# Recurrence steps traced 1000 places ahead of their own from the second group's round on, in a one-core decoder layer

## The chip, the cores and the metric

The program runs on one core of a Trainium2 chip. That core has a matrix engine (PE, with its weight loads shown apart as PEld), a vector engine (DVE), a scalar engine (ACT), a general engine (POOL) and a queue from which nearly all DMA transfers are issued (SP). Each engine works through its own instructions in the order in which the program lists them. The metric is the time of one execution in microseconds (us); lower is better. A difference of about 0.3%, some 10 us here, is the least that the measurement can tell from no change.

## What is computed

One decoder layer is applied to 1024 prompt positions and to 8 x 4 sample positions. Only the parts that matter here:

```python
z = rmsnorm(x) @ w_in
y_r = rwkv7_mix(z[..., :D_SHIFT], ...)    # a recurrence over positions
y_p = pool_mix(z[..., D_SHIFT:], ...)
h = x + concat([y_r, y_p]) @ w_out
h = h + peer_ffn(rmsnorm(h))              # top 16 of 16384 experts for each of 8 heads
h = h + (p @ ple_w) * sigmoid(rmsnorm(h) @ ple_gate_w)
y = rmsnorm(h)
```

The recurrence keeps a 64 x 64 state for each of 8 heads and updates it at every position, `s = s * w + s_kk (kk*a) + v k`, so it is serial along the prompt. `peer_ffn` projects to queries, scores them against two key tables, takes the best pairs, and sums the chosen experts' values with their gates.

## The kernel before

**Phase A** projects all 1056 positions and leaves the recurrence's inputs in DRAM (`fd`).

**The recurrence** is cut into 16 chunks of 64 prompt positions (`bchunk`, 17 calls with the sample positions). A chunk loads its inputs (`fdc`, L481), forms products and masks (`lp`, L492), inverts a triangular matrix by repeated products (`ltm`, `zp`, `yx`), takes the state of the chunk before it (`s_in = S[-1]`), writes a new state `S` (L595, L596), and normalizes and stores its rows (`yo` L617, `y_d` L619). Its matmuls are all recorded at L470. It is a Python generator of about 19 steps. `b_stream(ca, cb)` runs up to three chunks at a time (`NSLOT`), the next one started at least six steps (`STAG`) after the last, and it may start chunks up to two beyond `cb`.

**Phase C** (`phase_c(gi)`) takes one group of positions (`GROUPS`: 0..288, 288..544, 544..800, 800..1056): it loads `y_d` (L683), applies `w_out` (8 blocks), stores `h` and its normalized halves (`xh_d`, `xl_d`), applies `wq` (16 blocks) and the keys, and stores the scores `sc_d` (L743). Its matmuls are at L653 to L655, their weights come from `wc_d` (L642, L643) after the first group. Its tiles have one buffer, so the groups' phases run one after another. Chunks 0 to 3 belong to the first group with the sample positions, 4 to 7 to the second, 8 to 11 to the third, 12 to 15 to the fourth.

**The top stream** (`t_stream(gi)`) covers the first 672 positions in tiles of up to 128: it loads scores (`scq`, L758), picks the best on DVE (L761 to L766, `select`), and spreads the gates into a dense matrix: comparisons and products `ab` on DVE and POOL (L901, L902, L904), matmuls at L912, evictions `gst` on ACT (L913), and 2 MB stores `g_d` (L915).

**Rounds.** `merge` interleaves the streams in the trace, the one with the smallest finished share next. `BC = (0, 2, 4, 5, 8, 12, 16)` sets the chunks of each call: chunks 0 to 4 are traced beside the end of phase A, the sample positions and the pool's projection. Then come four rounds:

| round | recurrence | top stream | phase C |
|---|---|---|---|
| 1 | chunks 5 to 7 | | first group |
| 2 | 8 to 11 | first group | second group |
| 3 | 12 to 15 | second group | third group |
| 4 | | third group, up to 672 | fourth group, with 8 blocks of the dense stage |

After round 3 the recurrence's pools are closed (`pbx.close()`), and the dense stage's buffers (`dr`, `dps`) take their space: the loads of `XH` and `XL` (L1156, L1157), the first expert weights (`eraw<-uT`, L1092) and the dense matmuls (L1118) come behind the last chunk.

**The dense stage** works through all 16384 experts for the first 672 positions. Its first blocks need `XH` and `XL` only; the rest need the gates `gq` (from `g_d`), so the last `g_d` store of the third group. Beside it DVE and POOL gather experts for the last 384 positions.

**The order on each engine** is made when the program is built. Each instruction has a priority, its place in the trace; a planner runs a model of the chip's times, and whenever an engine is free there, it gives it the ready instruction with the smallest place. An instruction that isn't ready is passed over. What comes out is a fixed list for each engine and for the SP queue. `tc.high_priority(offset=n)` lowers the place of everything traced inside it by n.

Of the kernel before, what the change touches and what calls it, by code (L numbers as in the profile page):

```python
# [63 lines left out]
def body(ctx, tc, io):  # L64
# [852 lines left out]
    NG = len(GROUPS)  # L917
    NSLOT = 3
    STAG = 6

    active, nxt, since, held = [], [0], [0], [False]

    def b_stream(ca, cb, ahead=2):
        while nxt[0] < cb or any(c < cb for c, _ in active):
            c = nxt[0]
            if (c < min(cb + ahead, NCH) and len(active) < NSLOT and (not active or since[0] >= STAG)
                    and not (held[0] and c % NSLOT == 1)):
                active.append((c, bchunk(c)))
                nxt[0], since[0] = c + 1, 0
            since[0] += 1  # L930
            for a in list(active):
                try:
                    next(a[1])
                except StopIteration:
                    active.remove(a)
                yield

    def b_len(ca, cb):
# [29 lines left out]
    BC = (0, 2, 4, 5, 8, 12, 16)  # L968
    with tc.tile_pool(name="pa1", bufs=1) as pa1:
        with tc.tile_pool(name="pa", bufs=1) as pa:  # L970
            A = phase_a(pa1, pa)
            while next(A) is None:
                pass
        pb = pbx.enter_context(tc.tile_pool(name="pb", bufs=1, side="right", reuse_waits="tile"))
        id16 = pb.tile([128, 4, 64], F16, name="id16")
        for i in range(4):
            ACT(id16[:, i, :], ident2, AF.Copy)
        S = [pb.tile([128, 4, 64], F32, name="S", bufs=3)]

        def bzero():  # L980
            nc.gpsimd.memset(S[0], 0.0)

        bzero()
        merge([(16, A), (b_len(*BC[0:2]), b_stream(*BC[0:2]))])

    with tc.tile_pool(name="smp", bufs=1) as sp_, tc.tile_pool(name="hx", bufs=1) as hx:
# [67 lines left out]
        spf = sp_.tile([128, 28, 64], F32, name="spf")  # L1054
        nc.gpsimd.memset(spf, 0.0)
        merge([(30, sample(bchunk(-1, ((sp_, ssm), bmask, cmask, spf)))), (b_len(*BC[1:3]), b_stream(*BC[1:3]))])
        merge([(KB * (1 + T // XW), (x for st in (ple(), wpool()) for x in st)), (b_len(*BC[2:4]), b_stream(*BC[2:4]))])


# [343 lines left out]
def program(arrays, extra=()):  # L1403
    nc = bacc.Bacc("TRN2", target_bir_lowering=False, num_devices=1)
    io = {k: nc.dram_tensor(k, v.shape, mybir.dt.from_np(v.dtype), kind="ExternalInput").ap()
          for k, v in arrays.items()}
    for k, s in list(OUTS.items()) + list(extra):
        io[k] = nc.dram_tensor(k, s, F32, kind="ExternalOutput").ap()
    with tile.TileContext(nc, schedule_with_timeline_sim=True) as tc, ExitStack() as ctx:
        body(ctx, tc, io)  # L1410
    return nc
# [15 lines left out]
```

## Time and profile before

| | us |
|---|---|
| median of three runs | 3326.09 |
| lowest, highest of them | 3318.22, 3327.06 |
| the execution that was profiled | 3320.66 |
| its span, first to last instruction | 3318.5 |

A profile page shows each engine's busy time as a share of the span. A table of windows shows the same for stretches of the span, with the granted PE clock as a share of full speed and the share of the DMA engines' time in use. A chain of waits is followed back from the last instruction: each piece is what the next one waited for. In a timeline, the square bracket gives the idle time of the engine before a row and what ended it. The stages of the span:

| us from the start | stage |
|---|---|
| 0 to 520 | phase A, pool, sample positions, chunks 0 to 4 |
| 520 to 1350 | the four rounds, chunks 5 to 15 |
| 1350 to 3158 | dense stage |
| 3158 to 3318.5 | output stage |

### The profile page before, as it was taken

Reading aid. Unit: us, or ns where it says so; the run is one execution under the profiler, and the core shown is the slowest. Engines: PE = TensorE matmul, PEld = TensorE weight load, DVE = VectorE, ACT = ScalarE, POOL = GpSimd, SP = SyncE. Lnnn points to the kernel's source line nnn. Section 1 sums busy time; section 2 is a strip of 40 time slices with the busy share of each in tenths; the row PEclk is TensorE's granted clock in tenths of the full one; section 3 lists DMA queues with packets and bytes.
Section 4 is the critical chain, followed back from the end, with each engine's and each line's share of the span. In section 5 each row is a group of like instructions: output and inputs, shape, how many; then the busy total and the mean of one; then the engine's idle time right before and its main releaser. Section 6 shows DMA issues by size and latency. Waiting matters only on the chain.

```text
span 3318.5 us, 66499 instructions
## 1 busy us (share of the span) xinstructions
PE 3129.6 (94%) x26777; PEld 3000.2 (90%) x26777; DVE 2576.9 (78%) x4930; ACT 1129.7 (34%) x1732; POOL 1705.2 (51%) x1366
## 2 busy tenths in 40 slices
PE   8998898987988888999999999999999999999997
PEld 7886787876877787999999999999999999999997
DVE  7775333469599888789888888888888888888966
ACT  6442423434454555432222122222222222212243
POOL 5212232235464465247666665666566666666534
PEclk9999899988998988999999999999999999999998
DMA  3325557855776987559999899999999989999833
GB/s 117 117 87 128 149 142 230 278 176 173 213 214 200 282 260 224 198 209 350 341 350 328 325 354 331 328 343 339 330 336 353 329 326 341 333 332 340 309 109 127
DMA packets 437333, 858.89 MB, mean 259 GB/s; under 512 B 108960, under 2 KB 232096, under 8 KB 432544
## 3 DMA queue, kind: packets, MB, share of 16 engines
q1 hardware_dynamic: 326432, 451.93, 41.6%
q0 software_dynamic: 110592, 402.70, 33.0%
q8 instruction: 210, 3.44, 0.4%
q14 instruction: 99, 0.81, 0.1%
HBM read 733.92 MB, written 120.60 MB: 258 GB/s over the span
## 4 chain that ended last, share of the span: by engine, by line
PE 75%; DVE 12%; DMA 5%; issue 2%; ACT 2%; POOL 2%; SPq 1%; ACTq 0%; DVEq 0%; POOLq 0%
PE pd L1118 58%; PE ps L470 5%; PE ps L219 4%; DVE ab L901 2%; PE ps L653 2%; PE ps L655 2%; PE ps L654 2%; PE ps L302 1%; DMA whi<-wc_d 1%; PE ps L912 1%; DVE ab L902 1%; POOL ab L127 1%; DMA scq<-sc_d 1%; DVE ab L904 1%; DMA sc_d<-scs 1%
## 5 line engine op out<-in xcount | busy, mean ns | idle before, releaser
L1227 POOL DMA_INDIRECT row<-v,idx x384 | 542.9, 1414 | 313.7 <-DVE po L1244 154.0
L1227 POOL DMA_INDIRECT row<-u,idx x384 | 543.7, 1416 | 282.8 <-DVE row L1235 123.0
L1094 ACT ACTIVATE ehi<-eraw 128x1024 fp32r<-128x1024 f32 x278 | 294.9, 1061 | 1109.3 <-PE pd L1118 999.9
L1118 PE MATMUL pd<-XH,elo 128*128 128x336 f32 x2176 | 513.8, 317 | 2.4 <-DVE elo L1096 2.2
L1118 PE MATMUL pd<-XL,ehi 128*128 128x336 f32 x2176 | 514.4, 317 | 0.0
L1118 PE MATMUL pd<-XH,ehi 128*128 128x336 f32 x2176 | 512.5, 316 | 0.7 <-ACT ehi L1094 0.7
L1118 PE MATMUL pd<-wh,ehi 128*128 128x336 f32 (+1 forms) x2112 | 504.0, 317 | 6.3 <-DVE tg L1308 6.3
L1118 PE MATMUL pd<-wh,elo 128*128 128x336 f32 (+1 forms) x2112 | 503.9, 317 | 0.0
L1118 PE MATMUL pd<-wl,ehi 128*128 128x336 f32 (+1 forms) x2112 | 502.7, 317 | 0.0
L1244 DVE SCALAR_TENSOR_TENSOR po<-row,act,po 128x1024 f32<-128x1024 f32 x381 | 488.5, 1282 | 6.6 <-DMA row<-v,idx 0.2
L1235 DVE SCALAR_TENSOR_TENSOR row<-row,xt 128x1024 f32<-128x1024 f32 x384 | 455.0, 1219 | 8.3 <-DMA row<-u,idx 8.3
L1096 DVE TENSOR_TENSOR elo<-eraw,ehi 128x1024 fp32r<-128x1024 f32 x256 | 318.5, 1244 | 73.8 <-ACT ehi L1094 63.2
L1118 PEld LDWEIGHTS pd<-XH,elo 128*128 128x128 f32 x2176 | 373.0, 188 | 3.1 <-DVE elo L1096 2.7
L1118 PEld LDWEIGHTS pd<-XH,ehi 128*128 128x128 f32 x2176 | 372.7, 189 | 1.2 <-ACT ehi L1094 0.9
L1118 PEld LDWEIGHTS pd<-XL,ehi 128*128 128x128 f32 x2176 | 371.4, 188 | 0.2
L1118 PEld LDWEIGHTS pd<-wh,ehi 128*128 128x128 f32 x2112 | 362.5, 188 | 7.1 <-issue 6.9
L1118 PEld LDWEIGHTS pd<-wl,ehi 128*128 128x128 f32 x2112 | 362.7, 188 | 0.0
L1118 PEld LDWEIGHTS pd<-wh,elo 128*128 128x128 f32 x2112 | 361.9, 188 | 0.2
L653 PE MATMUL ps<-hi,whi 128*128 128x256 f32 (+1 forms) x592 | 189.1, 321 | 46.0 <-DMA whi<-wc_d 24.2
L1187 DVE TENSOR_TENSOR OT<-pd,OT 128x672 f32<-128x672 f32 x120 | 102.9, 858 | 148.5 <-PE pd L1118 147.5
L127 POOL TENSOR_TENSOR ab<-ab,e 128x512 f16<-128x512 f16 x110 | 143.5, 1317 | 135.3 <-DVE ab L902 96.4
L913 ACT ACTIVATE gst<-ps 128x512 f32<-128x512 f32 x168 | 174.2, 1098 | 94.9 <-PE ps L912 89.9
(427 smaller groups left out, 5431.2 us busy)
## 6 DMA issues: line engine op xcount, KB each, us to landing
eraw<-uT SPq DMA_DIRECT2D x128, 512.0 KB
eraw<-vP SPq DMA_DIRECT2D x128, 512.0 KB
g_d<-gst SPq DMA_DIRECT2D x21, 2048.0 KB
gq<-g_d SPq DMA_DIRECT2D x32, 1344.0 KB
whi<-wc_d SPq DMA_DIRECT2D x108, 256.0 KB
wlo<-wc_d SPq DMA_DIRECT2D x108, 256.0 KB
fdc<-fd SPq DMA_DIRECT2D x16, 896.0 KB
wc_d<-whi SPq DMA_DIRECT2D x40, 256.0 KB
```

The lines of the kernel that those rows point to most:

```text
L127: nc.gpsimd.tensor_tensor(out, a, b, op=op)
L219: mm(ps[:, :XW], s[:, k, :], x[:, k, a:b], start=first, stop=last)
L470: mm(o[hs], l[hs], r[hs], start=start, stop=stop)
L653: mm(ps[:, :n], whi[:, kk, :], xhi[:, k, :n], start=k == 0, stop=False)
L913: ACT(st[:, :, t2 + q:t2 + q + 4].rearrange("p e t -> p t e"), v3(ps, 128), AF.Copy, scale=1.0 / GS)
L1094: ACT(hi, raw, AF.Copy)
L1096: sub(lo, raw, hi.bitcast(F32), op=ALU.subtract)
L1118: mm(ps[:, a, :n], w_[:, k, :], x_[:, s:s + n], start=first, stop=last)
L1187: TT(halves(OT[db]), ps[:, :, :NH], halves(OT[db]), op=ALU.add)
L1227: nc.gpsimd.indirect_dma_start(out=r[:m], out_offset=None, in_=io[tab], in_offset=bass.IndirectOffsetOnAxis(ap=idx[:m, hh, k:k + 1], axis=0))
L1235: STT(r[:m], r[:m], 1.0, xt[:m], op0=ALU.mult, op1=ALU.mult, accum_out=pre[:m, k:k + 1])
L1244: STT(po[:m], r[:m], act[:m, k:k + 1], po[:m], op0=ALU.mult, op1=ALU.add)
```

## The change

`b_stream` gets a `with` around each single step of a chunk. For calls with `ca >= BC[3]` (= 5), so rounds 1 to 3, everything that the step traces (its matmuls, its work on DVE, ACT and POOL, its load of `fdc` and its store of `y_d`) has a place 1000 smaller than its own. The three calls before (chunks 0 to 4, and those steps of chunks 5 and 6 that these calls start ahead) keep their places, and so does every instruction of the other streams. `next(a[1], 0) == 0` is the end of the generator, as the caught `StopIteration` was. The order of the trace, the buffers, the arithmetic and the dependences are as before.

```diff
     STAG = 6
+    LEAD = 1000
...
             for a in list(active):
-                try:
-                    next(a[1])
-                except StopIteration:
-                    active.remove(a)
+                with tc.high_priority(offset=LEAD) if ca >= BC[3] else nullcontext():
+                    if next(a[1], 0) == 0:
+                        active.remove(a)
                 yield
```

## Prediction

> **What bounds the kernel now.** I read the table of windows first, to see which engine is full in which stage.
>
> ```profile
> core 0: us, PE busy (x) PEld busy (x) DVE busy (x) ACT busy (x) POOL busy (x), PEclk, DMA share, GB/s
> 520.00:690.00 170.00, 149.62 (x2286) 137.64 (x2282) 68.34 (x195) 69.79 (x151) 40.74 (x51) 0.93 0.82 268
> 690.00:850.00 160.00, 126.22 (x1790) 111.00 (x1789) 140.15 (x584) 69.80 (x129) 80.45 (x88) 0.85 0.62 180
> 850.00:900.00 50.00, 46.97 (x710) 43.10 (x709) 20.12 (x69) 17.64 (x37) 11.80 (x17) 0.97 0.79 227
> 900.00:1100.00 200.00, 174.27 (x2502) 151.68 (x2499) 185.92 (x664) 108.90 (x191) 112.00 (x112) 0.91 0.68 203
> 1100.00:1200.00 100.00, 83.32 (x813) 75.47 (x811) 75.86 (x159) 56.94 (x73) 50.39 (x39) 0.88 0.97 308
> 1200.00:1350.00 150.00, 128.69 (x1003) 121.14 (x1003) 121.59 (x522) 72.52 (x107) 82.36 (x68) 0.92 0.70 221
> 1366.60:3158.00 1791.40, 1791.40 (x11667) 1791.36 (x11666) 1566.40 (x2226) 447.40 (x541) 1107.28 (x793) 1.00 0.89 324
> ```
>
> From 1366.6 on PE has no gap for 1791.4 us: 11,667 matmuls at 153.5 ns. The change traces nothing there, so I keep that stage's length. What can move is when it begins. Before it, from 690 to 1350, DVE is busy 543.64 of 660 us (93% from 900 to 1100); its idle 116.4 us lie mainly at 850 to 900 (29.9), 1100 to 1200 (24.1) and 1200 to 1350 (28.4). Next, the chain of waits, for what the dense stage waited for:
>
> ```profile
> 1125.41 7.76 DMA sc_d<-scs
> ...
> 1333.88 10.60 DMA g_d<-gst
> 1344.54 5.66 DMA gq<-g_d
> ...
> 1366.60 653.85 PE pd L1118 x4256
> ```
>
> Backwards: the dense matmuls needed the gates, these the last `g_d` store at 1333.9, that the third group's tile in the top stream, and that the scores of the third group's phase C. The recurrence is not what phase C waits for. The SP queue shows it (start, length of the issue, line, transfer):
>
> ```profile
> 873.04 0.52 SPq L619 DMA_DIRECT2D y_d<-yo  x1
> 939.50 1.24 SPq L683 DMA_DIRECT2D y<-y_d  x1
> ...
> 1128.19 0.52 SPq L619 DMA_DIRECT2D y_d<-yo  x1
> 1134.55 0.42 SPq L1156 DMA_DIRECT2D XH<-xh_d  x1
> 1166.40 0.32 SPq L743 DMA_DIRECT2D sc_d<-scs  x1
> 1167.66 0.58 SPq L683 DMA_DIRECT2D y<-y_d  x1
> 1168.33 0.84 SPq L743 DMA_DIRECT2D sc_d<-scs  x1
> 1186.40 0.87 SPq L758 DMA_DIRECT2D scq<-sc_d  x1
> ```
>
> The third group's rows were stored at 873.0 and loaded at 939.5; the fourth group's at 1128.2 and 1167.7. Both times phase C of the group before still held the buffers, so the recurrence has 66 and 39 us to spare there. But two things stand behind its last chunk: the `XH` and `XL` loads begin only at 1134.55, 6 us after the last `y_d`, and run into the tail of the third group's phase C, whose last scores leave at 1168.33 and come back to the top stream at 1186.40.
>
> **The change part by part.** It adds and removes no work on any engine. It moves what 11 chunks issue.
>
> ```profile
> sum 830.00, PE 227.16 PEld 192.69; mean PE 45.43 PEld 38.54
> L595 DVE TENSOR_TENSOR S<-ps,S x16: 399/420/426, 345.1 to 1112.7; 128x256 f32<-128x256 f32 x16
> ...
> 757.09 0.41 DVE L595 TENSOR_TENSOR S<-ps,S 128x256 f32<-128x256 f32 x1
> 852.23 0.42 DVE L595 TENSOR_TENSOR S<-ps,S 128x256 f32<-128x256 f32 x1 [7.31 <-PE ps L470]
> ```
>
> The first row sums L470 over 520 to 1350: 227.16 us of PE for chunks 5 to 15, 20.7 us each. The states follow each other every 51 us on average ((1112.7 - 345.1) / 15), but the ninth and tenth change (counted from 0) are 95 us apart, in the stretch where DVE is full: there the recurrence has its turn behind older places. So there is something for a smaller place to act on.
>
> *The lead in time.* From 690 to 850 the four engines run 1790 + 584 + 129 + 88 = 2591 instructions in 160 us, 16.2 for each us; from 900 to 1100 it is 17.3. A thousand places are then about 60 us, somewhat more than one chunk. That is the upper bound; the lower one is nothing. I take 45 us, since a chunk still waits for its own chain and for the state before it, so the last `y_d` at 1083 in place of 1128.
>
> *What the lead takes from others.* Two rows of the SP queue, and the sizes of a chunk's transfers:
>
> ```profile
> 940.83 0.70 SPq L743 DMA_DIRECT2D sc_d<-scs  x1
> 996.34 0.38 SPq L915 DMA_DIRECT2D g_d<-gst  x1
> ...
> fdc<-fd SPq DMA_DIRECT2D x16, 896.0 KB
> y_d<-yo SPq DMA_DIRECT2D x16, 128.0 KB
> ```
>
> It is paid once, in rounds 1 and 2: one chunk's 20.7 us of PE come ahead of a phase C or top step. PE idles 20.4 us from 520 to 690 and 33.8 us from 690 to 850, and the second group's scores were early (the last left at 940.8, while the top stream was at the first group's tiles until its `g_d` at 996.3), so I cost it at nothing; without that cover it costs 20.7 us, since the groups' phases run one after another. The chunk's `fdc` loads and `y_d` stores go ahead on the SP queue too, 1 MB for a chunk (896 + 128 KB), while the DMA share is 0.62; I take nothing for these, and at most 1 MB at 180 GB/s, 6 us.
>
> *What it gives at the end of round 3.* The windows with all instructions, then with L470 alone, then the sizes of the loads behind the last chunk:
>
> ```profile
> 1083.00:1128.00 45.00, 38.14 (x520) 34.03 (x520) 36.70 (x76) 25.54 (x38) 22.18 (x18) 0.97 0.86 248
> 1128.00:1171.00 43.00, 32.41 (x290) 28.49 (x288) 34.73 (x60) 25.73 (x29) 18.65 (x14) 0.82 1.00 342
> ...
> 1083.00:1128.00 45.00, 12.34 (x256) 9.73 (x256) 0.97 0.86 248
> ...
> XH<-xh_d SPq DMA_DIRECT2D x8, 336.0 KB
> XL<-xl_d SPq DMA_DIRECT2D x8, 336.0 KB
> ```
>
> (a) 12.3 us of PE leave from between the third group's last blocks: up to 12 us earlier scores, nothing at the least. (b) The 16 loads of `XH` and `XL`, 336 KB each and 5.4 MB together, leave a stretch with DMA share 1.00 and 342 GB/s, where they took 16 us, for one at 248 GB/s; 45 us there have room for 4.2 MB, so 12 us of the 16 go, nothing at the least.
>
> Both shorten the same tail, and 24 us together are just DVE's idle from 1100 to 1200, which is the most that this stretch can give: behind it DVE is full with the tile. (c) Against it, the clock. Where PE had gaps it was granted less:
>
> ```profile
> 750.00:800.00 50.00, 34.30 (x381) 29.45 (x381) 49.97 (x214) 22.03 (x40) 24.55 (x31) 0.69 0.38 119
> ```
>
> PE busy 69% of the time got 0.69, and with 75% (1128 to 1171) 0.82. Without the recurrence, 1083 to 1128 holds 25.8 us of PE work; if its clock falls from 0.97 to 0.82, that work takes 4.7 us longer. The page "TensorE: Matmul & The Clock Gate" of the Trainium skill (What's actually happening) says that an idle window of about 3.4 us halves the clock until PE has been busy for as long; this rule speaks against clearing small matmuls out of a stretch, and the low clocks above agree with it. If the whole 45 us fell to half speed by that rule, the 25.8 us would cost some 24 us and eat the gain, an estimate from that page.
>
> *The sum*: 12 + 12 - 5 = 19 us earlier, 3320.66 - 19 = 3302 for the profiled execution. Its time lies 5.4 us under the median of 3326.09; the forecast for the median is 3326 - 19 = **3307 us**.
>
> **The rivals.**
>
> *No change (3326, within 10).* DVE's work is untouched and sets the pace; if the tail of phase C ends sooner, DVE only has its gaps elsewhere. The page "Perfetto Trace Analysis" of the Trainium skill (Identifying the Most-Contended Engine) would have it so: improve the fullest engine first, and that is DVE here. For it: DVE's 93% from 900 to 1100. Against it: the 24 idle us from 1100 to 1200. That the change doesn't do what it says belongs here too: if the chunks are held by their own chain and not by places, nothing moves. The 95 us between two states speak against that.
>
> *Slower (3347).* The recurrence's matmuls now stand ahead of phase C on PE, whose list is fixed: a chunk step that waits for ACT holds the matmuls behind it, and each group's phase follows the last one's. If the one chunk that is pulled forward isn't covered, the third group's scores come 20.7 us later, and the tile's `select` behind them: 3326 + 21 = 3347. It decides as soon as the last `sc_d` of the third group is issued after 1168. For it: in-order waits of this kind exist. DVE stood still for two of them:
>
> ```profile
> 864.15 0.42 DVE L603 TENSOR_REDUCE s<-ps 128x4 f32<-128x256 f32 x1 [11.03 <-PE ps L470]
> 883.45 0.09 DVE L762 MATCH_VALUE_LOAD I<-V,scq 128x8 f32 x1 [11.88 <-ACT F L775]
> ```
>
> Against it: PE's idle time in rounds 1 and 2 above.
>
> *Much faster (3277).* The same rows from the other side: if the recurrence has left 850 to 900 by the time that the first group's tiles are there, the 29.9 idle us of DVE close up as well: 3307 - 30 = 3277. Against it: the chunks form a continuous row, so another one will stand there.
>
> **How the numbers follow.** The forecast's mechanism with 10 to 30 us: 0.40. Much faster: 0.10. No change: 0.28. Slower by over 10 us: 0.22. So faster by over 0.3% (10 us, about what the measurement can tell from no change) 0.50, within 0.3% 0.28, slower 0.22. The order of all engines in rounds 1 to 4 is made anew, and stalls like the 11.03 and 11.88 us come and go by chance, one or two of them to either side. The range takes the forecast's own (3296 to 3316), no change, the nearer half of the slower cases up to 3340, and of the much faster ones those down to 3286. Left out: 0.1 above, 0.08 below.
>
> **What would show it.** Right: the last `y_d` is issued near 1083, `XH` 6 us behind it; the third group's last `sc_d` near 1149; the last `g_d` near 1315; PE without a gap from about 1348; the dense stage as long as before. Wrong, if the last `y_d` stays at 1128 (places do not hold the recurrence), if it comes early and the `sc_d` does not (phase C isn't held by it), or if `sc_d` comes early and the last `g_d` does not (DVE holds). What makes the whole forecast wrong is a new stall of 20 us on an in-order engine between 700 and 1350, which no row of before can show.

## The result and the profile after

| | before | after |
|---|---|---|
| median, us | 3324.97 | 3359.57 |
| lowest, highest of five runs | 3318.22, 3327.06 | 3357.53, 3362.5 |
| span of the profiled execution | 3318.5 | 3357.9 |

The ratio is 1.011, 95% interval 1.0097 to 1.0123: the change makes the kernel 1.1% slower, where 0.6% faster was forecast. Below is the table of windows of the changed kernel, cut as it was for the kernel before; the last window is its dense stage.

```profile
core 0: us, PE busy (x) PEld busy (x) DVE busy (x) ACT busy (x) POOL busy (x), PEclk, DMA share, GB/s
520.00:690.00 170.00, 153.90 (x2867) 141.68 (x2868) 62.95 (x153) 71.47 (x160) 50.04 (x66) 0.93 0.76 227
690.00:850.00 160.00, 139.03 (x1734) 122.04 (x1733) 127.96 (x591) 66.25 (x132) 65.25 (x75) 0.90 0.68 208
850.00:900.00 50.00, 49.05 (x534) 38.96 (x533) 23.46 (x70) 21.75 (x35) 18.20 (x23) 0.83 0.62 185
900.00:1100.00 200.00, 169.43 (x1933) 141.18 (x1931) 150.77 (x558) 88.94 (x157) 86.21 (x91) 0.86 0.66 210
1100.00:1200.00 100.00, 88.54 (x697) 82.75 (x698) 78.49 (x224) 49.66 (x63) 45.15 (x31) 0.86 0.75 228
...
1408.40:3198.00 1789.60, 1789.26 (x11635) 1788.49 (x11636) 1569.04 (x2228) 443.31 (x536) 1095.81 (x793) 1.00 0.90 325
```

The dense stage has the pace it had: 1789.60 us for 11,635 matmuls, 153.8 ns each (153.5 before). So the loss lies ahead of it. Up to 1200 the DVE column falls from 490.39 us (sum of the same five windows before) to 443.63. These 47 us of work that was not done by then answer to the 39 us by which the span grew, and 35 of them are missing between 900 and 1100 (185.92 before, 150.77 after), where DVE was 93% busy. In the same windows PE has fewer matmuls at a lower clock: 1933 at 0.86 in place of 2502 at 0.91.

The marks that the prediction named, from the SP queue of the changed kernel (start, length of the issue, line, transfer), with the load of the second group's rows ahead of them:

```profile
734.26 0.58 SPq L683 DMA_DIRECT2D y<-y_d  x1
...
1001.46 0.58 SPq L683 DMA_DIRECT2D y<-y_d  x1
...
1065.53 0.53 SPq L619 DMA_DIRECT2D y_d<-yo  x1
...
1070.15 0.32 SPq L1156 DMA_DIRECT2D XH<-xh_d  x1
...
1214.67 0.90 SPq L743 DMA_DIRECT2D sc_d<-scs  x1
...
1384.70 0.39 SPq L915 DMA_DIRECT2D g_d<-gst  x1
```

The recurrence did come early: its last `y_d` at 1065.5 (before 1128.2) and `XH` 4.6 us behind it. But the third group's rows are loaded at 1001.5 in place of 939.5, its last scores leave at 1214.7 in place of 1168.3, and the last `g_d` goes at 1384.7 in place of 1333.9. The loss was there at 1001, when the third group began: the third group's phase C itself is even shorter, 213 us (1214.7 - 1001.5) against 229. What became longer is the phase C of the second group, from its load at 734.3 to that of the third: 267 us against 244 (939.5 - 695.2). The first group's ends 39 us later, as the second group's load in the kernel before shows:

```profile
695.20 0.57 SPq L683 DMA_DIRECT2D y<-y_d  x1
```

### The profile page after: what moved, and what is told of

Read it like the earlier page. It is cut to its first block, busy times and chain, and to the rows that moved or that the text cites. A ratio compares the mean times of both kernels' runs of the same rounds, so it can differ in the third digit from the quotient of the medians.

```text
span 3357.9 us, 66519 instructions
## 1 busy us (share of the span) xinstructions
PE 3167.5 (94%) x26777; PEld 3021.7 (90%) x26777; DVE 2563.4 (76%) x4930; ACT 1127.7 (34%) x1729; POOL 1683.6 (50%) x1366
## 4 chain that ended last, share of the span: by engine, by line
PE 67%; DVE 9%; DMA 4%; ACT 1%; issue 1%; POOL 1%; SPq 0%; ACTq 0%; DVEq 0%; POOLq 0%
PE pd L1118 56%; PE ps L470 4%; PE ps L653 2%; PE ps L655 2%; PE ps L654 2%; PE ps L912 1%; DVE ab L901 1%; DMA scq<-sc_d 1%; DMA sc_d<-scs 1%; DMA whi<-wc_d 1%; DVE ab L902 1%; DVE h L710 1%; PE ps L739 1%; DVE I L762 1%; DVE s L764 0%
## 5 line engine op out<-in xcount | busy, mean ns | idle before, releaser
L1227 POOL DMA_INDIRECT row<-v,idx x384 | 533.7, 1390 | 320.4 <-DVE po L1244 152.6
L1118 PEld LDWEIGHTS pd<-wh,ehi 128*128 128x128 f32 x2112 | 363.2, 189 | 11.7 <-issue 6.8
L127 POOL TENSOR_TENSOR ab<-ab,e 128x512 f16<-128x512 f16 x110 | 129.8, 1192 | 189.7 <-DVE ab L902 165.2
```

The costliest lines, as they stand in the source:

```text
L127: nc.gpsimd.tensor_tensor(out, a, b, op=op)
L1118: mm(ps[:, a, :n], w_[:, k, :], x_[:, s:s + n], start=first, stop=last)
L1227: nc.gpsimd.indirect_dma_start(out=r[:m], out_offset=None, in_=io[tab], in_offset=bass.IndirectOffsetOnAxis(ap=idx[:m, hh, k:k + 1], axis=0))
```

## The experiments

Each one edits the changed kernel, unless it says otherwise. "Turns" below are the places in the list of PE's instructions, as built, where a 64x64 matmul of the recurrence (L470) follows one of another kind or is followed by it: 500 in the kernel before, 570 in the changed one.

### The rounds one by one, and in pairs

```diff
-                with tc.high_priority(offset=LEAD) if ca >= BC[3] else nullcontext():
+                with tc.high_priority(offset=LEAD) if ca == BC[3] else nullcontext():
```

> The lead of 1000 places is kept for round 1 alone (the call for chunks 5 to 7). Displacement theory: what costs is that the recurrence's matmuls go in front of the first group's phase C, whose y_d load for the second group then moves from 695 to about 734, and the groups' phases are one row that cannot catch up; so most of the 35 us show, 3345 to 3360, with the second group's y load near 730. Rival, early dense work: the XH loads and first dense blocks run into the third group's phase C; with the lead in round 1 alone the last chunk ends about as before, so 3325 within 10. Rival, chance: stalls appear anywhere, anything from 3310 to 3360, and not with a later y load of the second group.

Measured: 3286.74 us, ratio 0.9887 (0.9867 to 0.9907). With the lead in round 1 alone the kernel beats both others. The same edit with `ca == BC[4]` and with `ca == BC[5]` gives rounds 2 and 3 alone:

> The lead for round 2 alone (the call for chunks 8 to 11). Displacement theory: the steps go in front of the end of the first group's phase C and of the second group's; the y load of the third group moves from 939 by 20 to 40 us, the time is 3335 to 3350. Early dense work: 3325 within 10. Chance: no tie between the time and the third group's y load.

> The lead for round 3 alone (the call for chunks 12 to 15); the XH loads come earlier by 30 to 60 us, while phase C of the first two groups is left nearly alone. Displacement theory: little left to delay, since third group's phase C gains after the last chunk what it lost before: 3325 within 10, perhaps the 10 us gain of the prediction. Early dense work: this run has the whole cost, 3350 to 3360.

Measured: 3327.48 us (1.0011, 1.0001 to 1.0021) and 3327.38 us (1.0013, 1.0003 to 1.0023): each alone does almost nothing. Then in pairs, `ca in (BC[3], BC[4])` and `ca in (BC[3], BC[5])`:

> The lead in rounds 1 and 2, not in 3. Theory: the cost arises where the two leads meet. Round 2's call takes over chunks 8 and 9 that round 1's call has started, and with a lead of their own their steps get in front of the last blocks of the first group's phase C as well: 766 recurrence matmuls stand between 626 and 690 in the changed kernel, 308 with round 1 alone, and the second group's y load is 39 us late. Round 3 alone did nothing. So this run has the whole cost, 3350 to 3365, with the second group's y load near 734. Rival: each of the three leads is harmless or good alone and only all three together hurt, by the early dense stage; then 3285 to 3300 here.

> The lead in rounds 1 and 3, not in 2. Theory of the meeting leads: round 1's gain stays, 3280 to 3295, with the second group's y load near 693; the third round's lead only brings the XH loads forward. Rival, early dense stage on top of an early recurrence: 3325 to 3360 with XH near 1060.

Measured: 3300.35 us (0.9937, 0.992 to 0.9954) and 3318.42 us (0.9993, 0.9983 to 1.0003). Both theories that stood until here fell: no single round pays for a displaced chunk, and the leads of rounds 1 and 2 do not lose by meeting. The third round's lead costs 0.1% by itself, which is less than can be told from nothing, 1.1% on top of round 1, and 1.7% (3300 to 3360 us) on top of rounds 1 and 2.

Where round 1 gains shows in its table of windows:

```profile
520.00:690.00 170.00, 156.95 (x2534) 144.16 (x2536) 70.75 (x197) 75.07 (x163) 42.38 (x56) 0.97 0.85 269
...
850.00:900.00 50.00, 46.45 (x657) 41.27 (x658) 43.78 (x125) 30.28 (x52) 27.74 (x22) 0.93 0.77 220
```

PE does 2534 matmuls in the first stretch where the kernel before did 2286 (156.95 us against 149.62): room that was idle. DVE, which stood still for 29.9 us between 850 and 900, now works there for 43.78 us in place of 20.12. That is the hole of DVE whose closing the rival "much faster" had described. Its condition was not met, though: the recurrence has not left this stretch (376 of its matmuls there, 482 before), so what closed the hole is not shown.

The pair of rounds 1 and 2 and the changed kernel are alike up to 840 us (DVE 177.87 and 180.91 us from 520 on), so they can be laid side by side. First the run with rounds 1 and 2: two windows with all instructions, the same with L470 alone (PE and PEld only), and DVE's waits from 840 to 1000 (engine and line, what it waited for: us in total, times, longest):

```profile
840.00:1000.00 160.00, 141.00 (x1845) 122.92 (x1844) 139.25 (x459) 94.34 (x163) 95.73 (x91) 0.94 0.80 236
1000.00:1200.00 200.00, 168.57 (x1745) 152.34 (x1743) 181.03 (x669) 99.65 (x148) 102.14 (x93) 0.88 0.89 277
...
840.00:1000.00 160.00, 49.53 (x968) 38.93 (x968) 0.94 0.80 236
1000.00:1200.00 200.00, 23.23 (x534) 19.29 (x534) 0.88 0.89 277
...
DVE V L761 <- DMA scq<-sc_d: 12.9, 3, 8.0
DVE ab L901 <- PE ps L912: 4.3, 4, 2.3
```

The same views of the changed kernel, where the third round leads too, from 840 to 1000:

```profile
840.00:1000.00 160.00, 157.91 (x1748) 127.32 (x1749) 93.27 (x243) 71.75 (x120) 64.16 (x62) 0.84 0.56 165
...
840.00:1000.00 160.00, 77.37 (x1114) 55.56 (x1114) 0.84 0.56 165
...
DVE ab L901 <- PE ps L912: 28.0, 15, 7.7
DVE s L603 <- PE ps L470: 11.7, 2, 6.0
```

Here the time goes: DVE does 93.27 us of work in place of 139.25, and what it waits for is now PE, 28.0 us for the top stream's own matmuls (L912) and 11.7 us for the recurrence (one wait for ACT takes another 11.6 us). PE shows 157.91 of 160 us busy and yet does 97 matmuls fewer. The recurrence takes 77.37 us of it in place of 49.53, for only 15% more matmuls. So two things come together, more recurrence and dearer matmuls. The timeline of PE in the changed kernel shows what is dear (start, length, line, output and operands, array part, shape):

```profile
881.18 0.58 PE L653 MATMUL ps<-hi,whi 128*128 128x256 f32 x1
881.69 0.37 PE L470 MATMUL ps<-yx,ltm 64*64 64x64 f32 x1
...
881.85 0.31 PE L470 MATMUL ps<-yx,ltm 64*64 64x64 f32 x1
882.09 0.58 PE L654 MATMUL ps<-lo,whi 128*128 128x256 f32 x1
882.60 0.37 PE L470 MATMUL ps<-yx,ltm 64*64 64x64 f32 x1
...
882.77 0.31 PE L470 MATMUL ps<-yx,ltm 64*64 64x64 f32 x1
...
883.01 0.58 PE L655 MATMUL ps<-hi,wlo 128*128 128x256 f32 x1
```

Phase C's 128x128 matmuls and the recurrence's 64x64 ones take turns one by one, and each big one with the small ones behind it takes 0.92 us (882.09 to 883.01), at a granted clock of 0.50 (881 to 884). By the start times of the matmuls between 840 and 1000 there are 158 steps from L470 to a matmul other than L912 or back in the changed kernel, nearly all of them to or from phase C, 40.7 us from start to start, and 57 (17.7 us) in the run with rounds 1 and 2. With the top stream's L912 they are 258 (58.0 us) and 140 (37.2 us).

What this does to the second group's phase C can be read from its own load and that of the third group, first in the run with rounds 1 and 2. Behind them stands L470 between the two loads, in that run and in the changed kernel:

```profile
737.85 0.57 SPq L683 DMA_DIRECT2D y<-y_d  x1
...
941.41 0.64 SPq L683 DMA_DIRECT2D y<-y_d  x1
...
737.90:941.40 203.50, 66.49 (x1381) 54.66 (x1379) 0.92 0.74 217
...
734.30:1001.50 267.20, 114.74 (x1937) 87.48 (x1935) 0.86 0.60 176
```

With the lead in rounds 1 and 2 the second group's rows are loaded 43 us later than in the kernel before (737.9 against 695.2), as late as in the changed kernel. But its phase C then takes 204 us in place of 244, so the third group's rows come only 2 us late. With the third round's lead as well, 556 more matmuls of the recurrence run beside it, PE spends 48 us more on them, and it takes 267 us. These 64 us (267.2 - 203.6) are about the 59 us between the two times. Beside the 244 us of the kernel before ran 2011 of these matmuls, in 94.00 us of PE: against that kernel, this phase C grew by 23 us with fewer of them, which cost 21 us more.

### More and fewer leads

Phase C of the first three groups in the same lead as the recurrence, so that their order among themselves is nearly that of before:

```diff
+    def leading(g):
+        while True:
+            with tc.high_priority(offset=LEAD):
+                if next(g, 0) == 0:
+                    return
+            yield
...
-            streams.append((CL[step], phase_c(step - 1)))
+            streams.append((CL[step], leading(phase_c(step - 1)) if step < NG else phase_c(step - 1)))
```

> As the changed kernel, and phase C of the first three groups has the same lead of 1000 places, so that the recurrence is no longer ahead of it; the top stream is the one that now comes behind. Displacement theory: the y loads come back to 695 and 939 or earlier and the time to 3325 or below, 3300 to 3330. Early dense work: 3350 to 3360, since the last chunk is still early. Chance: anything.

Measured: 3500.4 us (1.0522, 1.0498 to 1.0545). It cures nothing and costs much; the list has 892 turns. Only the first group's phase C in the lead (`leading(phase_c(0)) if step == 1`):

> All leads as in the changed kernel, and the first group's phase C (round 1, the second, third and fourth as before) has the same lead of 1000 places, so that chunks 8 and 9 don't stand in front of it. Theory of the meeting leads: the second group's y load comes back to 690 to 700, and most of the 35 us are gone, 3290 to 3330. Rival: the cost lies in rounds 2 and 3 (second group's phase C took 267 us where it took 244), then 3340 to 3360 with an early second y load.

Measured: 3386.9 us (1.0198, 1.0181 to 1.0215). And without the lead for chunks 8 and 9 (`ca >= BC[3] and not (ca == BC[4] and a[0] < 10)`):

> The leads of the changed kernel, but the steps of chunks 8 and 9 that round 2's call traces keep their own places; chunks 10 and 11 lead. Theory of the meeting leads: no second chunk gets in front of the first group's phase C, so the second y load stays near 693 and the time is 3285 to 3330. Rival, cost in rounds 2 and 3: chunks 10 to 15 still lead, 3340 to 3360.

Measured: 3399.58 us (1.0234, 1.0206 to 1.0263): fewer steps lead and the loss doubles. All kernels that were over 1% slower so far were those with 570 turns and more. That made the turns the theory to test.

### The turns: by themselves, and kept away

192 matmuls of either kind, in five mixtures, with nothing else in the program:

> Measures the disputed cost by itself: leaves the whole computation out (its outputs are not the reference's) and runs 192 matmuls 128x128 on 128x256 (F32R) and 192 of 64x64 on 64x64 five times over, with turns every 192, 48, 8, 2 and 1 matmuls, after a warm-up each. Theory: with no turns about 192 x 0.12 + 192 x 0.045 = 32 us; with a turn at every matmul (383 turns, 0.33 and 0.19 us start to start) about 100 us, and a turn at every 8 about 43 us. Rival (a turn costs nothing by itself; the gaps of the changed kernel's trace are waits for operands): about 32 us in all of them.

The windows of its profile (one execution), one for each mixture, with a turn every 192, 48, 8, 2 and 1 matmuls (a 64x64 matmul of this type is two instructions, so 576 in each), and rows of PE's timeline in the last:

```profile
21.60:56.10 34.50, 34.50 (x578) 34.32 (x576) 0.00 (x0) 0.00 (x0) 0.00 (x0) 1.00 0.01 2
70.60:106.10 35.50, 35.50 (x579) 34.70 (x577) 0.00 (x0) 0.00 (x0) 0.00 (x0) 1.00 0.01 2
120.60:162.80 42.20, 42.20 (x579) 37.38 (x577) 0.00 (x0) 0.00 (x0) 0.00 (x0) 1.00 0.01 2
177.20:243.80 66.60, 66.60 (x579) 47.25 (x578) 0.00 (x0) 0.00 (x0) 0.00 (x0) 1.00 0.00 1
258.10:434.00 175.90, 172.69 (x578) 108.16 (x577) 0.76 (x2) 0.00 (x0) 0.00 (x0) 0.51 0.01 3
...
290.07 0.58 PE L84 MATMUL pb<-xhi,whi 128*128 128x256 f32 x1
290.58 0.47 PE L92 MATMUL pS<-yx,ltm 64*64 64x64 f32 x2
290.98 0.58 PE L84 MATMUL pb<-xhi,whi 128*128 128x256 f32 x1
```

A turn costs 0.17 us at the full clock: (66.60 - 34.50) / 190 with a turn every two, (42.20 - 34.50) / 46 with one every eight. One by one the granted clock falls to 0.51 of full speed, though PE is never idle, and the same work takes five times as long (172.69 against 34.50). A big and a small one take 0.91 us there (290.07 to 290.98), as the 0.92 in the changed kernel, where the clock was 0.50 too. Here no operand is waited for, so the 0.92 us need no such wait to explain them.

Keeping the 24 matmuls of a block of phase C together, in the changed kernel and, as a control, in the kernel before:

```diff
+    def mm3c(*a):
+        with tc.tile_critical():
+            mm3(*a)
...
-            mm3(ps, w, (yhi, ylo), n)
+            mm3c(ps, w, (yhi, ylo), n)
...
-                mm3(ps, w, (nhi, nlo), n)
+                mm3c(ps, w, (nhi, nlo), n)
```

> The change as it is, but the 24 matmuls of one block of phase C are kept together in PE's list, so that no recurrence matmul stands between two of them. In PE's list the turns between a 64x64 matmul of the recurrence and one of another shape fall from 570 (changed kernel; 500 in the kernel before) to 314. Theory (the change loses by the turns on PE at 840 to 1000 us): the second group's phase C takes about 210 us in place of 267 and the time is about 3300 us (3285 to 3315). Rival (the lead of three rounds puts recurrence work ahead of phase C, whatever their mixture): the second group's phase C stays at about 265 us and the time at 3350 to 3365.

> The kernel before, with the 24 matmuls of each block of phase C kept together: the control for the run with the change. The turns in PE's list fall from 500 to 438. Theory: 62 turns at about 0.26 us, 16 us of PE, not all of it on the path: 3308 to 3322 us. Rival (turns cost nothing, keeping the chains whole only holds recurrence matmuls up): 3320 to 3340.

Measured: 3925.35 us (1.1821, 1.1801 to 1.1841) and 3865.33 us (1.163, 1.1611 to 1.165). The means costs over 540 us in both, so this settles nothing, except that the control was needed.

### The length of the lead

`LEAD = 400`, then 300, 2000 and 3000, in all three rounds:

> The changed kernel with a lead of 400 places in place of 1000. A smaller lead should do less of what the change does, but PE's list has 778 turns in place of 570, 246 of them in one stretch of 500 matmuls in the first group's phase C. Theory (turns): slower than the changed kernel or as slow, 3355 to 3400 us, with the loss in the first group's phase C. Rival (the length of the lead is what costs): between the two kernels, 3320 to 3350 us.

> The changed kernel with a lead of 300 places; 1128 turns in PE's list, the most of all versions. Theory (turns): the slowest of the leads; from 570 turns at 3358 us and 778 at 3419, 0.30 us a turn, so about 3525 us (3470 to 3570), the granted clock at 600 to 900 us about 0.75. Rival (the length of the lead costs, and the run with 400 was slow by a chance of its order): 3320 to 3380 us, near the kernel before.

> The changed kernel with a lead of 2000 places; 470 turns in PE's list, 339 of them from the 5000th matmul on (the changed kernel 439, with a lead of 3000 it is 71). Theory (turns): between the runs with 1000 and 3000, 3300 to 3345 us. Rival (length of the lead): 3360 to 3400 us.

> The changed kernel with a lead of 3000 places in place of 1000, so that the recurrence goes ahead of phase C and top wholly. In PE's list the turns between a 64x64 matmul of the recurrence and one of another shape fall from 570 to 202 (kernel before: 500). Theory (turns): the loss goes although the lead is three times as long: 3270 to 3320 us, the second y load early (about 735 or before), the granted clock at 0.95 or more up to 1100 us. Rival (the lead puts recurrence work ahead of phase C and delays it): the longer the lead, the slower, 3370 to 3420 us.

| places of lead | turns in PE's list | median, us | ratio (interval) |
|---|---|---|---|
| 0 (before) | 500 | 3322.15 | |
| 300 | 1128 | 3506.26 | 1.056 (1.054 to 1.0579) |
| 400 | 778 | 3419.05 | 1.0293 (1.0273 to 1.0313) |
| 1000 (the change) | 570 | 3359.57 | 1.011 (1.0097 to 1.0123) |
| 2000 | 470 | 3381.47 | 1.0172 (1.0155 to 1.0189) |
| 3000 | 202 | 3369.94 | 1.0148 (1.0131 to 1.0165) |

The short leads bear the turns out: a lead that does less of what the change does is far slower, in the order of the turns, though with 400 places by more than the 3400 us allowed for. The window of the run with 400 places, where 246 of its turns fall close together:

```profile
600.00:800.00 200.00, 200.00 (x1526) 147.77 (x1522) 40.86 (x144) 44.45 (x91) 15.36 (x21) 0.70 0.40 131
```

and of the kernel before:

```profile
600.00:800.00 200.00, 165.29 (x2349) 150.95 (x2350) 134.17 (x645) 78.16 (x166) 61.56 (x81) 0.87 0.63 200
```

PE is full all the time at a clock of 0.70 and does 1526 matmuls where 2349 were done with time to spare; DVE, which works on what they produce, has 40.86 us of work in place of 134.17. More recurrence ahead is not the reason here: PE does fewer of its matmuls than before (1085 against 1692) and takes longer for them (96.86 us against 71.77). The second group's rows are loaded at 801.6 in place of 695.2. The long leads do not bear the turns out: 2000 places have fewer turns than the kernel before and are 1.7% slower, 3000 have the fewest and are still 1.5% slower. There it is the other theory, though not in proportion to the lead. The run with 3000 places:

```profile
640.00:740.00 100.00, 96.17 (x2027) 90.53 (x2024) 31.68 (x84) 41.42 (x93) 22.72 (x32) 0.99 0.59 167
740.00:840.00 100.00, 81.04 (x1446) 75.53 (x1448) 64.31 (x348) 33.86 (x79) 32.57 (x42) 0.86 0.32 104
```

2027 and 1446 matmuls, at a clock of 0.99 and 0.86, so PE is not slow here. But most of them are the recurrence's (1510 from 600 to 690, 1872 from 690 to 800; 782 and 910 before), the first group's phase C ends late (the second group's rows are loaded at 788.7 in place of 695.2), and DVE has 95.99 us of work in these 200 us, where the kernel before had 156.05 (58.32 and 97.73).

### The third round alone with another lead

Rounds 1 and 2 as in the change, the third with 3000 places, and in a second run with 600:

```diff
-                with tc.high_priority(offset=LEAD) if ca >= BC[3] else nullcontext():
+                with tc.high_priority(offset=LEAD if ca < BC[5] else 3000) if ca >= BC[3] else nullcontext():
```

> The changed kernel, but the third round leads by 3000 places in place of 1000; rounds 1 and 2 as in the change. The recurrence of the third round then goes ahead of the second group's phase C and top wholly and with few turns: from the 6000th matmul on 74 turns in PE's list in place of 314 (run with rounds 1 and 2 alone: 224). Theory A (turns on PE between 840 and 1000 us are what the third round's lead costs): the DVE is fed again in 840 to 1000 us, 3300 to 3330 us. Theory B (recurrence ahead of phase C is what it costs, with or without turns): as slow as the changed kernel or slower, 3350 to 3385 us, VectorE starved at 840 to 1000 us by matmuls of the recurrence that follow each other closely (over 1700 of them there, changed kernel 1114).

> The changed kernel, but the third round leads by 600 places in place of 1000. From the 6000th matmul on 296 turns in PE's list (changed kernel 314, with rounds 1 and 2 alone 224), spread later: 59, 94 and 87 per 500 matmuls in place of 144, 102 and 15. Theory A (turns): near the changed kernel, 3340 to 3360 us. Theory B (the amount of recurrence put ahead): about half way between the run with rounds 1 and 2 alone (3300) and the changed kernel (3358), 3315 to 3340 us.

Measured: 3353.66 us (1.0094, 1.0077 to 1.011) and 3340.32 us (1.0049, 1.003 to 1.0067). The windows of the run with 3000 places, all instructions and L470 alone:

```profile
840.00:1000.00 160.00, 131.42 (x2117) 120.26 (x2116) 104.94 (x284) 79.86 (x140) 74.31 (x70) 0.87 0.65 193
...
840.00:1000.00 160.00, 55.43 (x1415) 50.97 (x1413) 0.87 0.65 193
```

The turns are gone (55.43 us for 1415 small matmuls, 39 ns each; in the changed kernel 69 ns), and the time has hardly come back: DVE has 104.94 us of work, 93.27 in the changed kernel and 139.25 without the third round's lead. More recurrence stands ahead, 1415 matmuls against 968. Theory A fell, and theory B, the recurrence in front of phase C, accounts for this run, although the 1415 matmuls are fewer than the 1700 that it expected.

The median of the run with 600 places lies where the two theories' ranges meet, at 3340, so the time decides nothing between them. Its trace, of the slowest of its four executions (3350.57 us; the fastest took 3334.14), shows the other cause nearly by itself. Its windows, all instructions, then L470 alone:

```profile
840.00:1000.00 160.00, 144.70 (x1714) 123.08 (x1712) 116.67 (x360) 79.81 (x134) 73.58 (x77) 0.86 0.68 200
1000.00:1200.00 200.00, 167.87 (x1545) 144.64 (x1543) 147.87 (x507) 89.80 (x135) 83.85 (x77) 0.82 0.74 233
...
840.00:1000.00 160.00, 59.11 (x960) 45.87 (x960) 0.86 0.68 200
1000.00:1200.00 200.00, 34.26 (x534) 25.96 (x534) 0.82 0.74 233
```

It does as much recurrence in these two windows as the run with rounds 1 and 2 (960 and 534 matmuls against 968 and 534), and its last `y_d` leaves at 1110.3 against 1111.7, so hardly anything is put ahead. Yet these take 93.37 us in place of 72.76 (49.53 + 23.23), the clock is 0.86 and 0.82 in place of 0.94 and 0.88, and DVE has 264.54 us of work in place of 320.28. What differs is the mixture: from 820 to 1120 there are 290 turns by the trace's start times, 89.7 us from start to start, in the other run 220 (60.0 us).

### What all of them have in common

DVE's work between 520 and 1200 (one row of the table of windows for each run) against the ratio:

| run | DVE busy, us | ratio |
|---|---|---|
| round 1 | 517.14 | 0.9887 |
| rounds 1 and 2 | 498.15 | 0.9937 |
| before | 490.39 | 1 |
| round 3; rounds 1 and 3; round 2 | 485.86; 485.04; 472.80 | 1.0013; 0.9993; 1.0011 |
| third round with 3000; with 600 | 448.20; 446.14 | 1.0094; 1.0049 |
| the change | 443.63 | 1.011 |
| lead of 3000; of 2000 | 443.18; 437.07 | 1.0148; 1.0172 |
| first phase C leads; without chunks 8 and 9 | 432.91; 431.64 | 1.0198; 1.0234 |
| lead of 400; of 300; all three phases C lead | 417.16; 366.24; 312.13 | 1.0293; 1.056; 1.0522 |
| blocks kept together: changed kernel; kernel before | 246.23; 262.33 | 1.1821; 1.163 |

The less work DVE has got by 1200, the longer the kernel takes, with small exceptions: from the changed kernel to that with round 1 alone DVE's work there grows by 73.5 us and the median falls by 72.8. PE can set this, as it makes the scores that DVE works on. The table alone shows no cause; for the changed kernel the waits of DVE for PE, above, do, and for the other rows they are not shown here.

## Why the prediction was wrong

**The pace of the dense stage** was kept, as said (153.8 and 153.5 ns).

**The lead in time** was right in kind and somewhat too small: the last `y_d` came 62.7 us earlier (1128.2 to 1065.5), where 45 was taken and 60 was given as the upper bound. The doubt that the change doesn't do what it says is out. That 1000 places came so near to 60 us is partly luck: 16.5 us of the 62.7 come from rounds 1 and 2 (last `y_d` at 1111.7 with these alone) and 46.2 from the third, and 600 places in the third round moved it by 1.4 us, not by the 37 that 16.2 places for each us would give.

**What the lead takes from others** is the step that failed: "It is paid once, in rounds 1 and 2 ... so I cost it at nothing". For rounds 1 and 2 this was right in the outcome: both together are 0.6% faster, and round 1 alone 1.1%. It was not right in the way: with both, the first group's phase C does end 43 us later, twice the 20.7 us that were given as the cost without cover, and only a shorter phase C of the second group wins this back. And it is not paid once. With the lead in the third round as well more recurrence than with the first two enters the second group's phase C and the first group's top stream, at a time when PE has little left to spare (141.00 of 160 us busy from 840 to 1000 in the run with rounds 1 and 2), and nothing is won back. The cover named for it, PE's idle time from 520 to 850, was not used up: 37.5 us of the 54.2 are still there in the run with rounds 1 and 2, but ahead of the stretch that lost. The other cover, that the top stream is still at the first group's tiles when the second group's scores come, went with the tiles themselves: the first group's last `g_d` goes at 1038.1 in the changed kernel, at 997.0 with rounds 1 and 2 alone (996.3 before). The price of the third lead is 46 us of DVE's work (139.25 - 93.27) and 59 us of time.

Two mechanisms make it up, and each stands out in a run of its own: more recurrence ahead of phase C (the third round with 3000 places, few turns, 3354 us), and turns between 64x64 and 128x128 matmuls with a lower clock (the third round with 600 places, as much recurrence in these windows as without its lead, 3340 us). The first is shown; the second rests on that one trace, on the short leads and on the program with turns alone. The changed kernel has both, 146 more matmuls of the recurrence from 840 to 1000 and 101 more turns beside those with L912 there, 23 us from start to start. How much of its 59 us belongs to which is not settled: a longer lead that takes the turns away puts more recurrence ahead.

**The gains at the end of round 3** are a second step that failed, a term of 24 us that did not come. The run with the lead in round 3 alone tests it, as its third group starts on time (its rows are loaded at 936.0). Its last `y_d` and the last scores of its third group:

```profile
1073.74 0.52 SPq L619 DMA_DIRECT2D y_d<-yo  x1
...
1186.72 0.57 SPq L743 DMA_DIRECT2D sc_d<-scs  x1
```

The recurrence ends 54 us earlier than before, and the scores come 18 us later, where the forecast had them 19 us earlier; the time is 1.0013 of that before. The matmuls that left the end of this phase C had moved to its start: 1388 of the recurrence from 936 to 1187, 1378 in the kernel before (939.5 to 1168.3). Why it takes 251 us in place of 229 stays open. In the changed kernel: (a) The third group's phase C was to become up to 12 us shorter. It became 16 us shorter (229 to 213), behind a start that was 62 us late; that the matmuls which left it are the reason was not tested by itself, and in the run with rounds 1 and 2, where the recurrence goes on beside it up to 1111.7, it took 187 us. (b) `XH` came 64 us earlier, into another stretch than that reckoned with; whether its 12 us were won doesn't show. (c) The clock at 1100 to 1200 was 0.86 in place of 0.88, and in the 45 us that the prediction named (1083 to 1128) 0.70, where 0.82 was taken, with PE busy for 33.89 us; so a loss of this kind was there. The large one lay at 840 to 1000 (0.84), where PE was full and not idle.

**The rivals.** "Slower" named the mechanism (the recurrence's matmuls ahead of phase C), the side and the point, the third group's last `sc_d` after 1168: it came at 1214.7. Its price, one chunk of 20.7 us, was too small, as it counted the recurrence at the speed it had before and once. "Much faster" came near in the kernel with round 1 alone, 3287 us where 3277 was given, with DVE's hole closed, though not by the recurrence having left it. "What makes the whole forecast wrong" was put as a new stall on an in-order engine; it was none, but a stretch of 160 us in which PE had next to no idle time (2.09 us) and did less. "No change" fell with its reason, that DVE's work sets the pace: DVE was kept waiting and had 47 us less of it done by 1200.

## What to carry to other kernels

Ask of moved work not only whether the engine idles somewhere, but whether it idles where the work lands, each time that the move is made, and whether a delay is won back later: here the first round's lead was worth 1.1%, and the third's, on top of the first two, cost 1.7%. An engine that is shown 99% busy can be doing less than before; set the number of its instructions and the granted clock beside its busy time. And when two chains of matmuls with different array shapes are ready at once, a planner that mixes them one by one can make both slow; the number of turns can be counted in the built list before a run, but it is only a part of the price.

## What the runs showed of the hardware

The windows of the kernel with turns alone, for 120 matmuls of 128x256 in a row and for the stretch behind them, in which the turns are one by one:

```profile
243.80:258.10 14.30, 14.30 (x120) 14.30 (x121) 0.00 (x0) 0.00 (x0) 0.00 (x0) 1.00 0.00 1
258.10:275.00 16.90, 16.90 (x66) 10.68 (x65) 0.00 (x0) 0.00 (x0) 0.00 (x0) 0.63 0.00 0
275.00:285.00 10.00, 10.00 (x34) 6.29 (x33) 0.00 (x0) 0.00 (x0) 0.00 (x0) 0.50 0.00 0
```

A turn between a 64x64 and a 128x128 matmul took 0.17 us at the full clock, more than a whole 128x256 matmul in a row of its kind (14.30 us for 120, 0.12 us each). The two kinds differ in type as well (F32 and F32R), so which of the two costs the time is not shown. The page "TensorEngine Tiling (Array Packing)" of the Trainium skill (Key Properties) says that changing the tiling mode drains TensorE; the runs agree in that a turn costs time, but that a drain is what takes it they do not show. With turns one by one the granted clock fell to 0.50 within 17 us and stayed there, although PE shows no idle time; with turns every two it stayed at 1.00. The rule of "TensorE: Matmul & The Clock Gate" of the Trainium skill (What's actually happening), that an idle window halves the clock, doesn't tell the two apart, as PE shows no idle window in either. Why one mixture is throttled and the other is not, no run here shows.
